# A hybrid decoder block: the parameter chain loaded first and put on VectorE, the mixers' steps in another order, narrow PSUM outputs in the mixers

## The chip, the cores and the metric

The kernel runs on one core of one Trainium2 chip. The metric is the device time of one execution in microseconds (us). The core's engines are TensorE (PE in the profile, PEld for its weight loads), VectorE (DVE), ScalarE (ACT), GpSimd (POOL) and SyncE (SP, which issues most of the DMAs here). Every engine works through its own instructions strictly in order; they meet through semaphores.

## The reference, cut to what matters

One block over 256 positions with 2048 channels, fp32:

```python
proj = rmsnorm(x, norm1_g) @ w_in              # 2048 -> 3072: rg_u, rg_gate, s5_u
y_rg = rg_lru_group(rg_u, rg_gate, ...)        # conv of 4 taps, two gates per head, linear scan, gelu gate
y_s5 = s5_group(s5_u, s5_log_dt, s5_a_re, ...) # 64 groups of 64 complex states, linear scan, GLU
mixed = concat([rmsnorm(y_rg), rmsnorm(y_s5)])
x = x + mixed @ w_out                          # 2048 -> 2048
x = x + conv_gated_mlp(rmsnorm(x), ...)        # 2048 -> 2 x 6144 -> 2048, conv of 3 taps
return rmsnorm(x, final_norm_g)
```

The S5 group's state decays by `exp(A dt)` with `dt = exp(log_dt)`: a chain of small calculations on the parameters (an exponential, an angle reduced to one turn, sines, powers) comes before its first scan.

## The kernel before

**Products.** The activations lie with channels on partitions and 256 positions along the free axis. A product is one tile of 128 output channels: 16 steps of 128 input rows for w_in (24 tiles: 8 of rg_u, 8 of the gate, 8 of s5_u), 8 steps for each half of w_out (16 tiles by two halves) and for w_glu (8 tiles). fp32 accuracy comes from a split: the loaded weights `raw` are rounded into `wh` by ScalarE (`part`, L151) and `wl = raw - wh` is made by VectorE (L154); x is split in the same way. A step (`step`, L156 to L163) adds wh x_high, wh x_low and wl x_high. A *wide* step does the first two with one matmul of 512 columns into both halves of a PSUM bank (L159) and the third with one of 256 (L163); a *narrow* step puts all three into one half with three matmuls of 256 columns (L161 to L163). After a wide product `total` (L165 to L171) must add the two halves: a ScalarE copy (L169) and a VectorE add (L170). A narrow one is read from PSUM as it is. The string `WIDE` says, by letter, which products are wide; before, all of them are but w_down's last tile.

**Steps of the mixers.** Each has a letter and a tile number. U: a tile of rg_u with its convolution; P: its two gates; B: decay and input of the recurrence for four tiles; G: the gate's tile, the recurrence and their product; S: a tile of s5_u; X: the sines of the parameter chain; T (`s5_tables`): cosines and sines at every block of four positions for tile c, six GpSimd multiplications and additions (L495 to L497, each line for two results); K (`s5_mats`): the matrices of tile c, GpSimd work on `ball` (L515 to L517) and on `cp` (L524 to L528), then transposes `tp` (L535) and products `cb` (L541) on TensorE and eight small DMAs `u4` on SP's queue; N (`s5_scan`): `bu` on TensorE (L562) and ten or so VectorE instructions up to `wx` (L578, L579); Y (`s5_out`): the answers `y` on TensorE (L589 to L597) and one VectorE instruction (L599); F: gelu; Z: split; L: a tile of w_glu; W: the first half of a w_out tile; E: W's result times the norm and plus x; V: the second half; R, Q: the two norms' factors (`ss`, a square root, a reciprocal, `rb`). `ball` and its temporaries have one buffer, `cp` and its companions two, so K of tile c + 2 writes `cp` only behind Y of tile c.

**Parameter chain.** `exp_parts` (L324 to L366) makes dt from log_dt with some 50 small instructions on GpSimd; GpSimd goes on with the angles (L371 to L392), ScalarE makes the sines, VectorE prepares their arguments (up to L408) and does a second chain (L410 to L470).

**What sets the order.** The program is written as the steps stand in the string `ORDER`; that sequence gives each instruction its priority, and a scheduler that simulates the engines lays out each engine's own sequence from these priorities. The parameter chain is raised by a fixed offset (PRI). So an entry's place in ORDER is no time; it decides who goes first when an engine could take either.

The weights stream through four `raw` buffers, three of `wh` and of `wl`, by SP's queue. Behind the last V product the FFN follows with 96 + 16 longer products.

Of the kernel before, what the change touches and what calls it, by code (L numbers as in the profile page):

```python
# [14 lines left out]
P = 128  # L15
# [8 lines left out]
NST = 32  # L24
# [5 lines left out]
# The mixers' steps in the order of their priority: a letter of block_kernel's steps and a tile's number.  # L30
ORDER = """
U0 P0 S0 U1 P1 U2 S1 X0 U3 T0 T1 P2 P3 U4 U5 S2 B0 U6 P4 U7 S3 P5 S4 K0 P6 P7 T2 B1 K1 N0 N1 Y0 S5 T3 Y1 F0 G0
K2 G1 G2 S6 T4 G3 G4 K3 F1 N2 T5 Y2 N3 G5 G6 Y3 F2 G7 S7 F3 K4 N4 R0 K5 N5 W0 Y4 T6 W1 W2 Y5 K6 Z0 Z1 E0 E1 W3
E2 E3 Z2 K7 Z3 F4 W4 E4 F5 W5 E5 N6 W6 E6 W7 E7 T7 W8 E8 N7 Y6 W9 Y7 W10 W11 E9 Z4 F6 E10 E11 Z5 W12 F7 E12 Z6
Z7 L0 W13 E13 L1 W14 E14 L2 L3 W15 L4 E15 L5 L6 L7 Q0 V0 V1 V2 V3 V4 V5 V6 V7 V8 V9 V10 V11 V12 V13 V14 V15
"""
# The columns of w_in that the first loads feed, and the order of those loads: a quarter of x or a block of w_in.
# [11 lines left out]
def _top(v, bits):  # L49
# [10 lines left out]
    ("g1", KX), ("g2", KX), ("gf", KX),  # L60
# [3 lines left out]
    ("logdt", NST), ("lam", KH), ("are", NST), ("aim", NST),  # L64
    ("step", NX + NY), ("ident", P),
]
COL = {}
# [8 lines left out]
def block_kernel(ctx, tc, a, out):  # L76
# [9 lines left out]
    # ---------------------------------------------------------------- constants  # L86
    par = cpool.tile([P, NCOL], F32, name="par")
    S.dma_start(par[:, :KX], a["par"][:, :KX])
# [13 lines left out]
    WIDE = "FDAWVL"  # L102
# [13 lines left out]
    def fn(out, src, func, **kw):  # L116
        """An activation that needs its own table: these stay in program order, so that equal ones are neighbours."""
        ins = S.activation(out, src, func, **kw).ins  # L118
        if last_fn:
            tc.add_manual_dep(ins, last_fn[0].name, mybir.DependencyInfo(  # L120
                mybir.DependencyClass.NoSync, mybir.DependencyReason.DATA), reason="table order")
        last_fn[:] = [ins]

    # ------------------------------------------------------------- weight stream
    due = []

    def later(n, fn):
        """fn is emitted behind n more products."""
        due.append([n, fn])
# [26 lines left out]
    def step(ps, wide, wh, wl, kk, x, first, last):  # L156
        """Adds w.T x of 128 rows; wide puts w_high x_low beside the rest."""
# [15 lines left out]
    def product(src, ot, kcs, xs, wide=False):  # L173
        """w.T x; a caller that wants it in PSUM takes the narrow one."""
# [27 lines left out]
    def rstd(parts_, dim, tag):  # L202
        """1 / rms over the channels for every position, on all partitions; without a tag it stays in PSUM."""
# [17 lines left out]
    def rstd_direct(acc, dim, tag):  # L221
        """The same with one step on the tensor engine, more on the vector engine."""
# [17 lines left out]
    # ------------------------------------------------------------- split x  # L240
    # products that nobody reads raise the tensor engine's clock while the first loads run
# [5 lines left out]
    for name in HEAD_LOADS.split():  # L247
        if name == "p":
            nc.sync.dma_start(par[:, KX:], a["par"][:, KX:])
            continue  # L250
# [13 lines left out]
    # ===================================================================== mixers  # L264
    with ExitStack() as ph:
# [3 lines left out]
        # the first columns' products take turns by the rows of x, as these arrive  # L269
# [26 lines left out]
        # short steps let the chain of small ones on the parameters through  # L296
        pieces[0] = CUT

        # -------------------------------------------------- small parameter math
        ahead = tc.high_priority(offset=PRI)  # L300
        ahead.__enter__()
        # what the scans' tiles hold before them
# [12 lines left out]
        def stt(e, out, x, c, y, op0, op1):  # L315
            """(x op0 c) op1 y"""
# [46 lines left out]
        p0, s0, s1 = exp_parts(G, e_in, nE, "d")  # L363
        ex = tl(nE, "ex")
        stt(G, ex, p0, 1.0, s0, ALU.add, ALU.mult)
        G.tensor_tensor(ex, ex, s1, ALU.mult)  # L366
# [6 lines left out]
        # angle of one step, into [-pi, pi]  # L373
# [9 lines left out]
        # angle of a block of steps, in turns, as a short part and its rest; the four state tiles of a channel tile as s5_scan has them  # L383
# [9 lines left out]
        # cosine and sine at the multiples of NY blocks and at those below it  # L393
# [29 lines left out]
        # decay of a block, in s5_scan's order of the state tiles  # L423
# [7 lines left out]
        # powers 3, 2, 1 of A  # L431
# [13 lines left out]
        def times(ore, oim, xre_, xim_, yre, yim, t):  # L445
            """A product of complex numbers; t has the place of two."""
# [9 lines left out]
        # factors of b by the position in the block: A^(3 - position) (A - 1) / a; the real part negated as well  # L456
# [16 lines left out]
        # ------------------------------------------------------------ S5, by tile  # L473
        # Each block of positions is one step of the state's recurrence, in a frame that turns with it.
        # The four state tiles of a channel tile, 2 h + g, lie by g and then h.
        # The imaginary parts of b and of the state are carried negated.
        # What is zero off the diagonal: b [imaginary, tile, channel], c A^3 to c [power, imaginary, tile, channel],
        # the answers to u at the same block's positions [distance, channel]; and the decays, zero at the first block.
# [7 lines left out]
        def s5_tables(c):  # L486
            """Cosine and sine at every block."""
# [12 lines left out]
        def s5_mats(c):  # L500
# [7 lines left out]
            # b for the four positions, [imaginary, tile, channel, position]  # L508
# [386 lines left out]
```

## Time and profile before

| | us |
|---|---|
| median of 3 runs (lowest to highest) | 1183.16 (1183.14 to 1184.67) |
| profiled execution, span on the core | 1181.2 |
| TensorE busy in the span | 1119.9 (95%) |
| VectorE busy | 892.4 (76%) |
| ScalarE busy | 641.0 (54%) |
| GpSimd busy | 270.8 (23%) |

The span of the profiled execution is the time from its first to its last recorded instruction; the median of the runs lies 2.0 us above it, for what happens around it. Busy time is the time in which an instruction is recorded on the engine. A row of a timeline gives the start of an instruction, its duration, the engine, the line of the kernel, the operation, the tiles (output, then inputs), the shape, how many neighbours of the same kind are put together, and in brackets how long the engine was idle before and what released it. The table by windows gives for each engine the busy time and, in brackets, the number of instructions in the window, then the granted TensorE clock as a share of full speed, the share of the DMA engines' time and GB/s.

### The profile page before, as it was taken

To read this page: it belongs to the slowest core of one execution; us is meant where nothing else is said; L and a number is where in the kernel's file an instruction comes from. 1 tells how busy PE (TensorE), PEld (TensorE's weight loads), DVE (VectorE), ACT (ScalarE), POOL (GpSimd) and SP (SyncE) were. 2 spreads that over 40 slices of the span, in tenths; PEclk is the share of its full clock that TensorE was granted. 3 is DMA by queue.
4 is the path that set the end of the run, shared out by engine and by line. 5 is a ranking of instruction groups with operands and counts; after the bars stand their busy time and mean duration, and the time that the engine had idled before them with its cause. 6 is when DMAs were issued, how large, how long until landed. Compare 5 with 4: busy or idle time off the path is not lost.

```text
span 1181.2 us, 18986 instructions
## 1 busy us (share of the span) xinstructions
PE 1119.9 (95%) x7134; PEld 973.9 (82%) x7134; DVE 892.4 (76%) x1356; ACT 641.0 (54%) x1014; POOL 270.8 (23%) x300
## 2 busy tenths in 40 slices
PE   7887869879999999999999999999999999999996
PEld 6775658767888888888888888888888888888886
DVE  6899999997899887787787777877876444445443
ACT  6475655534876655555555555555554444344432
POOL 6368997893333000000000000000000000000000
PEclk8999889999999999999999999999999999999998
DMA  7554336443656666666666666666666666666662
GB/s 255 163 168 136 109 118 195 143 131 99 196 178 191 187 193 189 189 193 186 191 193 187 190 194 186 192 192 187 192 191 185 189 184 187 187 186 190 183 191 90
DMA packets 65980, 209.25 MB, mean 177 GB/s; under 512 B 12000, under 2 KB 15584, under 8 KB 65888
## 3 DMA queue, kind: packets, MB, share of 16 engines
q1 hardware_dynamic: 65744, 208.03, 58.5%
q8 instruction: 56, 0.92, 0.3%
q14 instruction: 36, 0.29, 0.1%
q10 hardware_dynamic: 144, 0.01, 0.0%
HBM read 204.87 MB, written 2.10 MB: 175 GB/s over the span
## 4 chain that ended last, share of the span: by engine, by line
PE 80%; POOL 9%; DVE 7%; issue 2%; ACT 1%; DMA 1%; SPq 0%; DVEq 0%; POOLq 0%; ACTq 0%
PE ps L159 51%; PE ps L163 27%; DVE wl L154 2%; POOL cp L528 1%; DVE wa L574 1%; POOL m L516 1%; POOL ball L517 1%; DVE xq L685 1%; ACT wh L151 1%; DMA xq<-in_xT 1%; POOL m L515 1%; POOL m L525 0%; PE ps L162 0%; DVE rcv L643 0%; PE ps L161 0%
## 5 line engine op out<-in xcount | busy, mean ns | idle before, releaser
L159 PE MATMUL ps<-sp,wh 128*128 128x512 f32 x2960 | 1043.9, 396 | 3.8 <-ACT wh L151 1.9
L163 PE MATMUL ps<-sp,wl 128*128 128x256 f32 x3008 | 851.3, 283 | 18.2 <-DVE wl L154 18.2
L159 PEld LDWEIGHTS ps<-sp,wh 128*128 128x128 f32 x2960 | 558.4, 189 | 130.0 <-DVE sp L199 2.5
L154 DVE TENSOR_TENSOR wl<-raw,wh 128x1024 fp32r<-128x1024 f32 (+2 forms) x384 | 478.5, 1248 | 234.4 <-ACT wh L151 232.7
L151 ACT CAST wh<-raw 128x1024 fp32r<-128x1024 f32 (+1 forms) x378 | 395.0, 1046 | 411.2 <-PE ps L159 286.2
L163 PEld LDWEIGHTS ps<-sp,wl 128*128 128x128 f32 x3008 | 572.3, 190 | 25.9 <-DVE wl L154 23.7
L236 POOL TENSOR_TENSOR accx<-accx,sq 128x256 f32<-128x256 f32 x29 | 37.7, 1301 | 793.6 <-ACT sq L235 793.5
L770 DVE SCALAR_TENSOR_TENSOR cv<-u,par,cv 128x255 f32<-128x255 f32 x192 | 92.1, 481 | 3.7 <-ACT cv L768 0.3
L170 DVE TENSOR_TENSOR t<-t,ps 128x256 f32<-128x256 f32 x160 | 65.7, 412 | 0.1
L169 ACT COPY t<-ps 128x256 f32<-128x256 f32 x160 | 57.8, 363 | 10.0 <-DVE u L720 7.6
L768 ACT ACTIVATE cv<-u,par 128x256 f32<-128x256 f32 x96 | 57.1, 596 | 1.4 <-DVE u L766 1.4
L766 DVE TENSOR_TENSOR u<-t,rstd 128x256 f32<-128x256 f32 x96 | 40.4, 421 | 1.6
L528 POOL TENSOR_TENSOR cp<-m,m 64x192 f32<-64x192 f32 x32 | 31.1, 973 | 1.9
L788 DVE TENSOR_TENSOR xq<-xq,ps 128x256 f32<-128x256 f32 x31 | 13.0, 421 | 16.4 <-PE ps L163 15.9
L721 POOL TENSOR_TENSOR xq<-xq,u 128x256 f32<-128x256 f32 x16 | 18.0, 1127 | 26.4 <-DVE u L720 20.8
L118 ACT ACT_TABLE_LOAD x17 | 21.8, 1283 | 1.4 <-PEq L884 1.2
L780 DVE TENSOR_TENSOR hv<-ge,cv 128x256 f32<-128x256 f32 x48 | 20.4, 426 | 1.9 <-issue 0.2
L118 ACT ACTIVATE ge<-cv 128x256 f32<-128x256 f32 x48 | 20.1, 419 | 0.2
L193 DVE TENSOR_TENSOR sp<-hv,sp 128x256 fp32r<-128x256 f32 x48 | 20.1, 419 | 0.0
L531 ACT COPY bp<-ball 64x128 f32<-64x128 f32 x16 | 6.8, 423 | 24.3 <-POOL ball L517 24.2
L192 ACT CAST sp<-hv 128x256 fp32r<-128x256 f32 x48 | 19.5, 406 | 0.0
L199 DVE SCALAR_TENSOR_TENSOR sp<-xq,par,sp 128x256 fp32r<-128x256 f32 x32 | 15.6, 521 | 1.5 <-ACT sp L198 1.5
(245 smaller groups left out, 654.2 us busy)
## 6 DMA issues: line engine op xcount, KB each, us to landing
raw<-in_w_up SPq DMA_DIRECT2D x192, 512.0 KB, 4.3
raw<-in_w_down SPq DMA_DIRECT2D x96, 512.0 KB, 4.3
raw<-in_w_in SPq DMA_DIRECT2D x47, 512.0 KB, 4.2
raw<-in_w_out SPq DMA_DIRECT2D x32, 512.0 KB, 4.1
raw<-in_w_glu SPq DMA_DIRECT2D x8, 512.0 KB, 4.1
xq<-in_xT SPq DMA_DIRECT2D x7, 512.0 KB, 6.0
out_y<-xq SPq DMA_DIRECT2D x6, 256.0 KB, 2.1
rw<-in_rgw SPq DMA_DIRECT2D x8, 128.0 KB, 3.5
```

The lines of the kernel that those rows point to most:

```text
L118: ins = S.activation(out, src, func, **kw).ins
L151: S.copy(wh[:, k, :], raw[:, k, :])
L154: V.tensor_tensor(wl[:, i:i + n, :], raw[:, i:i + n, :], wh[:, i:i + n, :].bitcast(F32), ALU.subtract)
L159: PE.matmul(ps, lhsT=wh[:, kk, :], rhs=x, start=first, stop=False)
L163: PE.matmul(ps[:, 0, :], lhsT=wl[:, kk, :], rhs=x[:, 0, :], start=False, stop=last)
L169: S.copy(t, ps[:, 1, :])
L170: V.tensor_tensor(t, t, ps[:, 0, :], ALU.add)
L236: G.tensor_tensor(acc, acc, q, ALU.add)
L528: G.tensor_tensor(cp[rp, :BL - 1, m, :, 16 * h:16 * h + 16], m1[rp], m2[rp], op)
L766: V.tensor_tensor(u, ps, rs["n2"], ALU.mult)
L768: S.activation(cv, u, AF.Identity, bias=col("fcb", o), scale=col("fcw", 2 * 2 * KF + o))
L770: V.scalar_tensor_tensor(cv[:, d:], u[:, :T - d], col("fcw", (2 - d) * 2 * KF + o), cv[:, d:], ALU.mult, ALU.add)
```

## The change

1. The columns of `par` are reordered. The first DMA (ScalarE's queue) loads the norm's gains and now log_dt, lambda, the real and imaginary parts of A and the step numbers with them (136 columns instead of 16); the rest follows on SP's queue with 632 columns instead of 752, at the same place.
2. `exp_parts` and the two instructions behind it get `V` (VectorE) where they had `G` (GpSimd).
3. `ORDER` is another sequence.
4. `WIDE` keeps only the FFN's letters: the 24 products of w_in, the 32 of w_out and the 8 of w_glu become narrow, 64 in all, and lose L169 and L170. What read `t` reads PSUM.

Comments and docstrings go too, and all line numbers from L88 on rise by one.

```diff
 ORDER = """
-U0 P0 S0 U1 P1 U2 S1 X0 U3 T0 T1 P2 P3 U4 U5 S2 B0 U6 P4 U7 S3 P5 S4 K0 P6 P7 T2 B1 K1 N0 N1 Y0 S5 T3 Y1 F0 G0
-K2 G1 G2 S6 T4 G3 G4 K3 F1 N2 T5 Y2 N3 G5 G6 Y3 F2 G7 S7 F3 K4 N4 R0 K5 N5 W0 Y4 T6 W1 W2 Y5 K6 Z0 Z1 E0 E1 W3
...
+U0 X0 S0 P0 U1 P1 T0 K0 U2 P2 S1 N0 Y0 U3 P3 B0 T1 K1 U4 P4 S2 N1 Y1 U5 P5 T2 K2 U6 P6 S3 N2 Y2 U7 P7 B1 T3 K3 F0
+F1 F2 G0 S4 N3 Y3 F3 T4 K4 G1 G2 S5 N4 Y4 F4 T5 K5 G3 G4 S6 N5 Y5 F5 T6 K6 G5 G6 S7 N6 Y6 F6 T7 K7 G7 N7 Y7 F7 R0
...
-    ("g1", KX), ("g2", KX), ("gf", KX),
+    ("g1", KX), ("logdt", NST), ("lam", KH), ("are", NST), ("aim", NST), ("step", NX + NY),
+    ("g2", KX), ("gf", KX),
...
-    ("logdt", NST), ("lam", KH), ("are", NST), ("aim", NST),
-    ("step", NX + NY), ("ident", P),
+    ("ident", P),
...
+NFIRST = KX + 3 * NST + KH + NX + NY
...
-    S.dma_start(par[:, :KX], a["par"][:, :KX])
+    S.dma_start(par[:, :NFIRST], a["par"][:, :NFIRST])
...
-    WIDE = "FDAWVL"
+    WIDE = "FD"
...
-            nc.sync.dma_start(par[:, KX:], a["par"][:, KX:])
+            nc.sync.dma_start(par[:, NFIRST:], a["par"][:, NFIRST:])
...
-        p0, s0, s1 = exp_parts(G, e_in, nE, "d")
+        p0, s0, s1 = exp_parts(V, e_in, nE, "d")
         ex = tl(nE, "ex")
-        stt(G, ex, p0, 1.0, s0, ALU.add, ALU.mult)
-        G.tensor_tensor(ex, ex, s1, ALU.mult)
+        stt(V, ex, p0, 1.0, s0, ALU.add, ALU.mult)
+        V.tensor_tensor(ex, ex, s1, ALU.mult)
```

Three places show what the scheduler makes of it. First GpSimd at the start of the program, between the sums of squares of x (`acc_130`, L289) and the angles (`room`, L371 before, L372 after). Before:

```order
L289 TENSOR_TENSOR acc_130<-acc_130,q 128x1024
L332 TENSOR_SCALAR room<-room 128x40
L333 TENSOR_SCALAR room<-room 128x40
L334 TENSOR_SCALAR room<-room 128x40
L321 TENSOR_SCALAR room<-room 128x40
L349 TENSOR_SCALAR room<-room 128x40
```

The exponential begins there and the first angle instruction stands 28 rows further on. On the same engine after:

```order
L290 TENSOR_TENSOR acc_130<-acc_130,q 128x1024 x2
L372 TENSOR_TENSOR room<-par,room 128x32
L373 TENSOR_TENSOR room<-par,room 128x32
L376 TENSOR_SCALAR room<-room 128x32
L377 TENSOR_SCALAR room<-room 128x32
```

The exponential has left GpSimd; the angles stand right behind the sums, and wait for VectorE's dt.

Second TensorE around the first W products. Before, the matrices of tile 4 (`cb_2416`, `bu_2438`) stand inside W1 (`ps_2637`):

```order
L159 MATMUL ps_2637<-sp_2166,wh_2640 128x512
L541 MATMUL cb_2416<-cp0_511,bp0_510 32x96 x8
L562 MATMUL bu_2438<-u4_2429,bt_2414 64x64 x16
L163 MATMUL ps_2637<-sp_2166,wl_2641 128x256
L159 MATMUL ps_2637<-sp_2227,wh_2640 128x512
L163 MATMUL ps_2637<-sp_2227,wl_2641 128x256
L159 MATMUL ps_2637<-sp_2326,wh_2640 128x512
```

The same engine after, at the first W product (`ps_3223` is W0, `ps_3070` is G7, `bu_3144` belongs to tile 7, the last):

```order
L162 MATMUL ps_3070<-sp_315,wh_3103 128x256
L163 MATMUL ps_3070<-sp_315,wh_3103 128x256
L164 MATMUL ps_3070<-sp_315,wl_3104 128x256
L563 MATMUL bu_3144<-u4_3061,bt_3046 64x64 x16
L162 MATMUL ps_3223<-sp_1827,wh_3226 128x256
L163 MATMUL ps_3223<-sp_1827,wh_3226 128x256
L164 MATMUL ps_3223<-sp_1827,wl_3227 128x256
```

Before, W0 to W9 stand between the matrices of tiles 4 to 7; after, no W product stands ahead of the last matrices, and the gates' products G0 to G7 with S5 to S7 fill those places.

Third TensorE and VectorE around the answers of tile 3 (`y_1923`) and the matrices of tile 4 (`cb_2007`), after. TensorE:

```order
L542 MATMUL cb_2007<-cp0_571,bp0_570 32x96 x4
L162 MATMUL ps_2177<-sp_133,wh_2180 128x256
L590 MATMUL y_1923<-wx_1912,cp1_579 32x64 x8
L593 MATMUL y_1923<-us3_1523,cb1_580 128x192
L593 MATMUL y_1923<-us3_1523,cb1_580 128x128
L593 MATMUL y_1923<-us3_1523,cb1_580 128x64
L598 MATMUL y_1923<-wx_1912,cp1_579 32x63 x24
```

and VectorE, where `y_1923` is read:

```order
L155 TENSOR_TENSOR wl_2181<-raw_2178,wh_2180 128x1024
L600 SCALAR_TENSOR_TENSOR us2_1171<-us2_1171,par_70,y_1555 128x256
L155 TENSOR_TENSOR wl_2211<-raw_2208,wh_2210 128x1024
L155 TENSOR_TENSOR wl_2380<-raw_2377,wh_2379 128x1024
L600 SCALAR_TENSOR_TENSOR us3_1523<-us3_1523,par_70,y_1923 128x256
L673 TENSOR_SCALAR q4_1670<-e4_1669 128x1024
L674 TENSOR_SCALAR e4_1669<-tau_1102 128x1024
```

The answers of a tile stand on TensorE behind the `cb` of the next tile, which is the last thing that the next tile's GpSimd work feeds; on VectorE the weights' subtractions of later products stand behind the instruction that reads these answers. The same pattern repeats at tiles 0, 2, 4 and 5.

## Rows read from the trace of the kernel before

**Rows 1.** Page: span, and shares of the chain that ended last

```profile
span 1181.2 us, 18986 instructions
...
PE 80%; POOL 9%; DVE 7%; issue 2%; ACT 1%; DMA 1%; SPq 0%; DVEq 0%; POOLq 0%; ACTq 0%
```

**Rows 2.** Windows: start, end, length, busy (count) PE PEld DVE ACT POOL, PEclk, DMA

```profile
0.00:60.00 60.00, 49.55 (x252) 41.46 (x253) 44.18 (x115) 32.40 (x49) 31.79 (x69) 0.94 0.62 208
```

**Rows 3.** Windows: from the first table to the last K; all mixers

```profile
70.30:271.70 201.40, 161.58 (x1469) 133.03 (x1468) 189.53 (x244) 110.46 (x210) 182.06 (x185) 0.93 0.44 135
...
0.00:364.30 364.30, 313.10 (x2459) 263.22 (x2460) 327.60 (x528) 215.32 (x394) 246.87 (x282) 0.95 0.51 158
```

**Rows 4.** TensorE's waits before 360 us: engine, line, releaser, total, times, longest

```profile
PE ps L163 <- DVE wl L154: 18.2, 17, 3.1
PE cb L541 <- POOL cp L528: 8.8, 3, 6.6
```

**Rows 5.** Timeline of POOL: first angle, first table, first K, end of the last K

```profile
33.28 0.25 POOL L371 TENSOR_TENSOR room<-par,room 128x32 f32<-128x32 f32 x1
...
70.33 0.70 POOL L496 TENSOR_TENSOR tm<-xs 128x256 f32<-128x256 f32 x1
...
91.73 0.65 POOL L515 TENSOR_TENSOR m<-pk,fr 128x256 f32<-128x256 f32 x1 [2.73 <-DVE fr L451]
...
270.12 1.60 POOL L528 TENSOR_TENSOR cp<-m,m 64x192 f32<-64x192 f32 x2
```

**Rows 6.** Timeline of DVE and ACT: the sines' argument, a small instruction, the sines

```profile
61.82 0.40 DVE L408 TENSOR_SCALAR xs<-xs 128x512 f32<-128x512 f32 x1
62.15 0.17 DVE L418 TENSOR_TENSOR room<-room 128x32 f32<-128x32 f32 x1
...
68.33 1.28 ACT L118 ACT_TABLE_LOAD   x1
69.62 0.63 ACT L118 ACTIVATE xs<-xs 128x512 f32<-128x512 f32 x1
```

**Rows 7.** Timeline of PE: W0; matrices of K4; answers; a V product; FFN

```profile
218.19 0.48 PE L159 MATMUL ps<-sp,wh 128*128 128x512 f32 x1
...
224.37 0.54 PE L541 MATMUL cb<-cp,bp 128*32 128x96 f32 x16
224.84 0.69 PE L562 MATMUL bu<-u,bt 64*64 64x64 f32 x32
...
284.67 0.43 PE L589 MATMUL y<-wx,cp 128*32 128x64 f32 x16
...
286.74 0.39 PE L163 MATMUL ps<-sp,wl 128*128 128x256 f32 x1
...
333.78 0.39 PE L159 MATMUL ps<-sp,wh 128*128 128x512 f32 x1
...
336.56 0.39 PE L159 MATMUL ps<-sp,wh 128*128 128x512 f32 x1
...
364.29 0.39 PE L159 MATMUL ps<-sp,wh 128*128 128x512 f32 x1
```

**Rows 8.** Narrow steps of w_down's last tile (durations, starts); two wide starts, 48 steps apart

```profile
L161 PE MATMUL ps<-sp,wh x48: 279/279/279, 1152.1 to 1168.7; 128*128 128x256 f32 x48
...
1119.63 0.40 PE L159 MATMUL ps<-sp,wh 128*128 128x512 f32 x1
...
1136.59 0.40 PE L159 MATMUL ps<-sp,wh 128*128 128x512 f32 x1
```

**Rows 9.** Windows with L154 alone: with GpSimd busy beside it, and without

```profile
70.00:272.00 202.00, 64.98 (x40) 0.93 0.44 134
600.00:800.00 200.00, 88.55 (x73) 1.00 0.65 190
```

**Rows 10.** Windows with L170 alone, the same two stretches

```profile
70.00:272.00 202.00, 10.12 (x25) 0.93 0.44 134
600.00:800.00 200.00, 14.91 (x36) 1.00 0.65 190
```

More of the change, by code (lines that the diff above doesn't have):

```diff
@@ L31 @@
 ORDER = """
-U0 P0 S0 U1 P1 U2 S1 X0 U3 T0 T1 P2 P3 U4 U5 S2 B0 U6 P4 U7 S3 P5 S4 K0 P6 P7 T2 B1 K1 N0 N1 Y0 S5 T3 Y1 F0 G0
-K2 G1 G2 S6 T4 G3 G4 K3 F1 N2 T5 Y2 N3 G5 G6 Y3 F2 G7 S7 F3 K4 N4 R0 K5 N5 W0 Y4 T6 W1 W2 Y5 K6 Z0 Z1 E0 E1 W3
-E2 E3 Z2 K7 Z3 F4 W4 E4 F5 W5 E5 N6 W6 E6 W7 E7 T7 W8 E8 N7 Y6 W9 Y7 W10 W11 E9 Z4 F6 E10 E11 Z5 W12 F7 E12 Z6
-Z7 L0 W13 E13 L1 W14 E14 L2 L3 W15 L4 E15 L5 L6 L7 Q0 V0 V1 V2 V3 V4 V5 V6 V7 V8 V9 V10 V11 V12 V13 V14 V15
+U0 X0 S0 P0 U1 P1 T0 K0 U2 P2 S1 N0 Y0 U3 P3 B0 T1 K1 U4 P4 S2 N1 Y1 U5 P5 T2 K2 U6 P6 S3 N2 Y2 U7 P7 B1 T3 K3 F0
+F1 F2 G0 S4 N3 Y3 F3 T4 K4 G1 G2 S5 N4 Y4 F4 T5 K5 G3 G4 S6 N5 Y5 F5 T6 K6 G5 G6 S7 N6 Y6 F6 T7 K7 G7 N7 Y7 F7 R0
+W0 Z0 Z1 E0 W1 Z2 Z3 E1 W2 Z4 Z5 E2 W3 Z6 Z7 E3 L0 L1 W4 E4 L2 L3 W5 E5 L4 L5 W6 E6 L6 L7 W7 E7 W8 E8 W9 E9 Q0 W10
+E10 W11 E11 W12 E12 W13 E13 W14 E14 W15 E15 V0 V1 V2 V3 V4 V5 V6 V7 V8 V9 V10 V11 V12 V13 V14 V15
 """
```

## The prediction

> **What bounds the kernel now.** The page comes first: a span of 1181.2 us, and on the chain that ended last PE has 80%, POOL 9% and DVE 7% [rows 1]. POOL does nothing in the FFN, so its 9% lie in the mixers. The table by windows says where: of the first 60 us PE is busy for 49.55 and DVE for 44.18 [rows 2]; over the whole mixers, which end with the first FFN matmul at 364.29 [rows 7], PE is busy for 313.10 of 364.30 us [rows 3]. Between the first table (70.33) and the end of the last K (271.7) POOL is busy for 182.06 of 201.40 us and DVE for 189.53 [rows 3, 5]: here these two set the pace and PE follows. The table of PE's waits says the same: wl of DVE holds it 17 times, 18.2 us in all, and cp of POOL 8.8 us [rows 4]. PE's own clock is part of it: 0.93 in that stretch, 1.00 where it is always fed. After 364.3 nothing changes. So the whole prediction is the time at which the mixers end, T, and the time after is T + (1181.2 - 364.3) + 2.0 = T + 818.9; the 2.0 are what the median, 1183.16, has over the span.
>
> **Part 1: parameters first, exponential on DVE.** The longer first load moves 128 x 120 x 4 bytes = 61 KB more ahead; at the 208 GB/s of the first 60 us [rows 2] that is 0.3 us on another queue, while DVE still has nothing to split. Taken as nothing. POOL loses the exponential and had dt ready at 33.28 [rows 5]. DVE gains 51 instructions of 40 elements. Its small ones take 0.17 us [rows 6], so 8.7 us, in a stretch in which it was idle for 60 - 44.18 = 15.8 us [rows 2]: that idle time is the cover, and without it the weights behind the chain come up to 8.7 us later. When do the sines come? DVE's sequence now has 124 instructions up to the sines' argument (which started at 61.82 [rows 6]): 51 small ones, 8.7 us, and 73 others at the mean 44.18/115 = 0.384, 28.0 us. With all of the 15.8 us idle that is 52, with none 37; I take 50, since part of the old idle time was waiting that the chain now fills. The sines follow (0.63 us each with their hand-overs, and no load of a table directly ahead, which cost 1.28 [rows 6]): 3 us. **The tables start at 53** instead of 70.33, between 47 and 60. The first K follows 21 POOL instructions later, at about 74 instead of 91.73.
>
> **Part 2: the order.** What a 17 us earlier start is worth is decided by what stands behind it. Before, W0 starts at 218.19 [rows 7], and ten W products lie between the matrices of the last four tiles, so PE has work while POOL finishes. After, no W product stands ahead of the last matrices. All 40 w_out and w_glu products come behind one point, W0, and T is W0 plus their work. So POOL's rate fixes W0. From the first table to the end of K6 it has 160 instructions. At 182.06/185 = 0.984 us each [rows 3] they take 157.5 and end at 210.5; at 201.40/185 = 1.089, the old waits included, 174 and 227. Part of the old waits were for the old order's interleaving, but the new one has waits of its own (below). I take the middle, **219**.
>
> From K6's end to W0 PE has, in its order: cb 0.5, 46 matmuls of 256 columns, the answers of tile 5, 63 matmuls, bu, tp, 26 matmuls, cb, 22 matmuls, bu. A matmul of 256 columns is a third of a narrow step, and a step is 16.6/47 = 0.353 [rows 8], so 0.118; cb and bu are 0.5 and 0.7, the answers 286.74 - 284.67 = 2.1 [rows 7], tp like cb. Sum: 157 x 0.118 = 18.5, and 5.0 for the rest: 23.5. Added wait: the answers of tile 5 need N5, whose last instruction is DVE's 209th from the start of the tables. At DVE's 189.53/244 = 0.777 that is 215, at 201.40/244 = 0.825 it is 225.5; PE wants it at 225. But in the new order DVE also waits: the reading of y_1923 stands ahead of the rest on DVE, y_1923 stands on PE behind cb of K4, and that behind POOL; queued behind it on DVE are B1, u and wl of the next w_in products, for which PE waits in turn. I take 4 (0 to 9). **W0: 219 + 23.5 + 4 = 246.5.**
>
> From W0 on PE is fed: 40 products of 8 steps, 336.56 - 333.78 = 2.78 each [rows 7], 111.2; two sets of answers, 4.1; the two norms' small matmuls, like two bu, 1.4. W3's wl stands on DVE behind the reciprocal of R, and this behind the answers of tile 7, a square root and a table load: an estimate of 5 us (3 to 8) in which PE has nothing else. Sum 121.7, and **T = 368.2**, where it was 364.3: the 17 us of earlier tables go into 40 products that no longer fill gaps.
>
> **Part 3: narrow outputs.** PE: a narrow step of 0.353 [rows 8] against wide ones of 2.78/8 = 0.3475 in the mixers [rows 7]. Over 704 steps the difference is 3.9 us; but in the same place as the narrow steps, 48 wide ones take 1136.59 - 1119.63 = 16.96, again 0.353 [rows 8]. That row is the nearest; I take nothing and keep 0 to 4, and no gain, for the columns are the same. DVE and ACT lose 64 additions and copies; the additions took 10.12/25 = 0.405 [rows 10], 26 us in all. From W0 on PE is the bound and these are covered. Before W0 DVE loses 24 of them, which is in the count of 209 already.
>
> Does a lighter DVE make POOL quicker? wl, which reads raw and wh, takes 64.98/40 = 1.62 beside a busy POOL and 88.55/73 = 1.21 without one [rows 9]; L170, which reads t and a PSUM bank, 0.405 and 14.91/36 = 0.414 [rows 10]. So the removed additions were not in POOL's way. But u, the product of t and rstd1, now reads PSUM in place of t, and becomes such an instruction. (The Trainium skill, page "SBUF — State Buffer", section "Who interferes with whom", says it as a rule: a VectorE instruction with two SBUF inputs contends with a GpSimd one that reads SBUF, the pair of ports being held for the whole instruction; one with a single SBUF input does not. The two rows agree with it in kind; by it the 64 additions gave POOL nothing, and the sum stands, while the u's help it, which is the first rival.)
>
> **Rivals.**
> *Faster: the u's stop blocking POOL.* Some 18 u's lie between the first table and K6's end. If each cost POOL its whole duration, of the size of L170's 0.41, K6 ends 18 x 0.41 = 7.4 us earlier, at 211.6, and DVE is early enough for the answers of tile 5 (the 4 us go): 1187.1 - 11.4 = 1175.7, say **1176**. With the half of the waits that I kept gone as well, 1168. It decides when K6 ends before 212.7, since the time is K6's end + 968.1. For it: [rows 9, 10]. Against it: 7.4 us is a bound, for POOL is not beside every u, and the B1 and N instructions are as many as before.
> *No change:* K6 ends between 212.7 and 217.4: 1180.8 to 1185.5. It needs only 2 to 6 us from my 219, well inside its ends.
> *The chain does not come earlier.* DVE's head is busier than I think, the sines wait for it as before (61.82), the tables start at 60: 7 us later, **1194**; with POOL's slower rate, 227, it is 1202. It is the case in which the change doesn't do what it says. Against it: DVE's idle 15.8 us.
> *Narrow steps cost PE* the upper bound, 320 x 0.0055 = 1.8 us behind W0: **1189**.
>
> **How the numbers follow.** The forecast is 219 + 968.1 = **1187**, with the slower neighbours up to 1194 (also the narrow steps): 0.37. The chain late or POOL at its slow rate, 1194 and over: 0.13. No change: 0.18. Faster: 0.32. A measurement of this kernel can tell about 0.2%, 2.4 us, from no change, so the bounds are 1180.8 and 1185.5: faster 0.32, same 0.18, slower 0.50. Of the faster case little lies below 1168 (0.08) and of the slow one about as much above 1202; the range is 1168 to 1202. The forecast's own range is 1185 to 1194.
>
> **What will show it.** In the changed kernel's profile: the first table on POOL at 53 (47 to 60); the first K at 74; the last instruction of K6 at 219 and of K7 at about 237; DVE idle for several us ahead of the reading of tile 3's answers; the first W product on PE at 246.5, right behind a bu; from there 122 us with PE solid but for a hole of about 5 us ahead of W3; the first FFN product at 368. No copy or addition of two PSUM halves before the FFN, and the FFN as long as before, 816.9 us. The prediction is wrong if K6 ends before 213 (POOL or its waits cheaper than counted), if PE waits much longer than 4 us for tile 5's answers, or if a narrow step shows over 0.353 at full clock.

## The result

The changed kernel takes 1194.66 us (median of four runs, 1192.53 to 1195.09) against 1183.74 us before: a ratio of 1.0085, 95% interval 1.0071 to 1.0100. It is slower by 10.9 us, where 4 were forecast. In the profiled execution the first FFN matmul starts at 373.9 us instead of 364.3 [rows 7], and the FFN takes what it took: 1190.7 - 373.9 = 816.8 us. So the loss lies in the mixers, as the forecast had it, and it is larger.

The page of the changed kernel, span and chain, to be read beside [rows 1]; DVE has 9% of the chain and POOL 5%, where it was 7% and 9%:

```profile
span 1190.7 us, 20225 instructions
...
PE 81%; DVE 9%; POOL 5%; issue 2%; ACT 1%; DMA 1%; SPq 0%; DVEq 0%; POOLq 0%; ACTq 0%
```

Its timeline of POOL (start, duration, engine, line, operation, tiles; lines are one higher than before): the first table, the first instruction of the first K, the last one of tile 6 and of tile 7. They answer to [rows 5].

```profile
49.96 0.89 POOL L497 TENSOR_TENSOR tm<-xs 128x256 f32<-128x256 f32 x1 [13.48 <-ACT xs L119]
...
73.24 1.87 POOL L516 TENSOR_TENSOR m<-pk,fr 128x256 f32<-128x256 f32 x1 [2.96 <-DVE fr L452]
...
217.46 1.26 POOL L529 TENSOR_TENSOR cp<-m,m 64x192 f32<-64x192 f32 x2
...
234.66 2.14 POOL L529 TENSOR_TENSOR cp<-m,m 64x192 f32<-64x192 f32 x2
```

The tables start 20 us earlier than before, and the last K ends at 236.8 instead of 271.7. And yet the mixers end 9.6 us later. PE's timeline shows the rest: the last bu and W0 behind it, rb and W3, the first step of V1 and the first of V2 (8 steps later), the first FFN matmul. They answer to [rows 7].

```profile
247.22 1.24 PE L563 MATMUL bu<-u,bt 64*64 64x64 f32 x32
248.39 0.39 PE L162 MATMUL ps<-sp,wh 128*128 128x256 f32 x1
...
263.36 0.71 PE L215 MATMUL rb<-par,rs 128*128 128x128 f32 x4 [1.11 <-DVE rs L212]
264.09 0.39 PE L162 MATMUL ps<-sp,wh 128*128 128x256 f32 x1
...
330.73 0.28 PE L162 MATMUL ps<-sp,wh 128*128 128x256 f32 x1
...
333.61 0.28 PE L162 MATMUL ps<-sp,wh 128*128 128x256 f32 x1
...
373.93 0.40 PE L160 MATMUL ps<-sp,wh 128*128 128x512 f32 x1
```

A narrow product of 8 steps takes 333.61 - 330.73 = 2.88 us here; the wide one took 2.78 [rows 7].

Two views account for the 9.6 us. The first is the table by windows from PE's first product (7 us) to the first third matmul of the FFN, 364.5 before and 374.2 after (start, end, length, then busy time and count of PE, PEld, DVE, ACT, POOL, the granted clock, DMA share, GB/s). Before:

```profile
7.00:364.50 357.50, 308.46 (x2435) 258.75 (x2436) 325.31 (x522) 211.48 (x388) 242.74 (x267) 0.95 0.51 157
```

After:

```profile
7.00:374.20 367.20, 325.03 (x3140) 309.17 (x3141) 315.03 (x486) 194.76 (x328) 224.24 (x240) 0.93 0.48 154
```

PE is idle for 49.0 us before and 42.2 after, so it gained 6.8 there; but it is busy for 16.6 us more. By an estimate, about 7 of these are clock (0.95 against 0.93, 0.02 of 367 us: more of the time at the lower of the two levels, 1.2 instead of 2.4 GHz), and about 9 the narrow steps, 704 x 0.0125 = 8.8 (0.360 us for a narrow step here, 0.3475 for a wide one). The second view is the same table with the third matmul of a step alone (L163 before, L164 after), whose count is the number of steps done. Before:

```profile
0.00:120.00 120.00, 66.07 (x222) 43.68 (x222) 0.96 0.56 178
120.00:180.00 60.00, 25.98 (x86) 17.80 (x87) 0.88 0.40 124
180.00:240.00 60.00, 33.84 (x118) 22.33 (x117) 0.97 0.53 165
```

After:

```profile
0.00:120.00 120.00, 55.95 (x183) 38.61 (x183) 0.91 0.50 164
120.00:180.00 60.00, 26.85 (x85) 18.49 (x85) 0.87 0.40 123
180.00:240.00 60.00, 30.43 (x101) 20.66 (x100) 0.91 0.43 135
```

By 240 us PE had done 426 of the mixers' 704 steps before, and 369 after: 57 steps, 20 us, fewer, 39 of them by 120 us already. The window up to there, before and then after:

```profile
0.00:240.00 240.00, 197.67 (x1473) 163.62 (x1473) 216.21 (x349) 136.84 (x240) 186.80 (x221) 0.94 0.51 161
...
0.00:240.00 240.00, 197.94 (x1938) 183.88 (x1942) 208.39 (x346) 123.28 (x213) 189.36 (x217) 0.90 0.46 147
```

PE was busy equally long, so the earlier matrices had brought no idle time back by then. By an estimate from these rows, the lower clock takes half of the 20 us (0.04 x 240 = 9.6), the price of the narrow steps 4.6 (369 x 0.0125), and only the rest, some 6 us, is the matrices and answers of early tiles, which PE did ahead of products. That part is not lost, since it need not be done later, and the 6.8 us of idle time are won behind 240 us; so the end moves by less than the 20 us.

### The profile page after: what moved, and what is told of

The parts are those of the page before. It is cut to its first block, busy times and chain, and to the rows that moved or that the text cites. A ratio compares the mean times of both kernels' runs of the same rounds, so it can differ in the third digit from the quotient of the medians.

```text
span 1190.7 us, 20225 instructions
## 1 busy us (share of the span) xinstructions
PE 1136.6 (95%) x7838; PEld 1024.5 (86%) x7838; DVE 878.0 (74%) x1318; ACT 622.4 (52%) x947; POOL 247.2 (21%) x270
## 3 DMA queue, kind: packets, MB, share of 16 engines
q1 hardware_dynamic: 65744, 207.97, 54.3%
## 4 chain that ended last, share of the span: by engine, by line
PE 81%; DVE 9%; POOL 5%; issue 2%; ACT 1%; DMA 1%; SPq 0%; DVEq 0%; POOLq 0%; ACTq 0%
PE ps L160 43%; PE ps L164 27%; PE ps L162 4%; PE ps L163 4%; DVE wl L155 2%; POOL cp L529 1%; DMA xq<-in_xT 1%; DVE xq L686 1%; DVE rcv L644 1%; POOL ball L518 1%; DVE wa L575 1%; POOL m L516 1%; POOL m L517 1%; DVE sp L200 0%; POOL m L525 0%
## 5 line engine op out<-in xcount | busy, mean ns | idle before, releaser
L164 PE MATMUL ps<-sp,wl 128*128 128x256 f32 x3008 | 855.9, 285 | 13.9 <-DVE wl L155 13.9
L160 PE MATMUL ps<-sp,wh 128*128 128x512 f32 x2256 | 787.1, 393 | 0.0
L164 PEld LDWEIGHTS ps<-sp,wl 128*128 128x128 f32 x3008 | 577.3, 192 | 17.0 <-DVE wl L155 15.8
L160 PEld LDWEIGHTS ps<-sp,wh 128*128 128x128 f32 x2256 | 422.6, 187 | 95.6
L162 PE MATMUL ps<-sp,wh 128*128 128x256 f32 x752 | 222.3, 296 | 7.3 <-ACT wh L152 4.6
L163 PE MATMUL ps<-sp,wh 128*128 128x256 f32 x752 | 221.2, 294 | 0.1
L162 PEld LDWEIGHTS ps<-sp,wh 128*128 128x128 f32 x752 | 151.8, 202 | 9.8 <-ACT wh L152 5.8
L163 PEld LDWEIGHTS ps<-sp,wh 128*128 128x128 f32 x752 | 151.6, 202 | 0.9 <-DVE sp L200 0.5
L171 DVE TENSOR_TENSOR t<-t,ps 128x256 f32<-128x256 f32 x96 | 39.7, 413 | 0.0
L170 ACT COPY t<-ps 128x256 f32<-128x256 f32 x96 | 34.7, 361 | 0.0
L529 POOL TENSOR_TENSOR cp<-m,m 64x192 f32<-64x192 f32 x32 | 26.4, 825 | 4.9 <-PE y L598 3.0
L200 DVE SCALAR_TENSOR_TENSOR sp<-xq,par,sp 128x256 fp32r<-128x256 f32 x32 | 21.9, 703 | 0.5 <-ACT sp L199 0.5
L781 DVE TENSOR_TENSOR hv<-ge,cv 128x256 f32<-128x256 f32 x48 | 20.4, 425 | 1.7
```

Of the source, the lines that this page charges most:

```text
L160: PE.matmul(ps, lhsT=wh[:, kk, :], rhs=x, start=first, stop=False)
L162: PE.matmul(ps[:, 0, :], lhsT=wh[:, kk, :], rhs=x[:, 0, :], start=first, stop=False)
L163: PE.matmul(ps[:, 0, :], lhsT=wh[:, kk, :], rhs=x[:, 1, :], start=False, stop=False)
L164: PE.matmul(ps[:, 0, :], lhsT=wl[:, kk, :], rhs=x[:, 0, :], start=False, stop=last)
L171: V.tensor_tensor(t, t, ps[:, 0, :], ALU.add)
L529: G.tensor_tensor(cp[rp, :BL - 1, m, :, 16 * h:16 * h + 16], m1[rp], m2[rp], op)
```

## The experiments

Two theories stood against each other. The first is the prediction's: the earlier chain is a gain, the new order turns it into a loss since all 40 products of w_out and w_glu stand behind one point, and the narrow outputs cost a little PE time where PE is the bound. The rival: the order is harmless, and narrow outputs or the meeting of VectorE and GpSimd make the time. All ratios are to the kernel before on the same chip.

| kernel | us | ratio, 95% interval | mixers' end | w_up |
|---|---|---|---|---|
| before | 1183.74 | | 364.5 | 533.4 |
| chain alone | 1182.75 | 0.9995 (0.9986 to 1.0004) | 365.3 | 533.5 |
| order alone | 1208.43 | 1.0209 (1.0193 to 1.0225) | 380.2 | 543.4 |
| narrow alone | 1181.86 | 0.9990 (0.9979 to 1.0000) | 363.6 | 533.5 |
| chain, order | 1204.94 | 1.0176 (1.0160 to 1.0191) | 376.6 | 543.4 |
| chain, narrow | 1180.14 | 0.9970 (0.9953 to 0.9987) | 362.4 | 533.5 |
| chain, w_in narrow | 1180.78 | 0.9967 (0.9954 to 0.9980) | 362.0 | 533.5 |
| chain, order, w_in narrow | 1200.54 | 1.0148 (1.0133 to 1.0163) | 372.5 | 543.4 |
| the change: chain, order, narrow | 1194.66 | 1.0085 (1.0071 to 1.0100) | 374.2 | 533.5 |
| the change with a third order | 1193.43 | 1.0078 (1.0061 to 1.0095) | 374.2 | 533.5 |

The mixers' end is the start of the FFN's first third matmul, w_up the time from there to w_down's, both from the traces. Four pairs of rows differ by the order alone, and in all four it makes the mixers longer: 364.5 to 380.2, 365.3 to 376.6, 362.4 to 374.2, and 362.0 to 372.5, which is 10 to 16 us. Of the eight combinations of the three parts, order with narrow outputs alone was not run.

**Each part alone.** The chain alone: the changed kernel with the old order (its beginning is shown) and wide mixers:

```diff
-U0 X0 S0 P0 U1 P1 T0 K0 U2 P2 S1 N0 Y0 U3 P3 ...
+U0 P0 S0 U1 P1 U2 S1 X0 U3 T0 T1 P2 P3 U4 U5 ...
...
-    WIDE = "FD"
+    WIDE = "FDAWVL"
```

> The kernel before with the parameter chain of the change alone: parameters first, exponential on VectorE; old order, wide mixers. Theory (the chain is a gain and the order gives it away): the first table starts at about 50 as in the changed kernel instead of 70.3, W products still lie between the last matrices, the mixers end 8 to 20 us earlier than 364.3, time 1164 to 1176. Rival (GpSimd and VectorE set the pace and an earlier start only makes them meet more often): the tables start early, the last K ends within 3 us of 271.7, time 1181 to 1187.

Measured: no difference, 0.9995. The step that failed is the start of the tables. In POOL's timeline it is 67.07, not 50:

```profile
67.07 0.67 POOL L497 TENSOR_TENSOR tm<-xs 128x256 f32<-128x256 f32 x1 [0.41 <-ACT xs L119]
```

In the old order X0 stands behind the first gates. The sines' argument is ready on VectorE at 51.6, but ScalarE is busy with the gates and with weights until 65.1 and only then turns to the sines. The order alone (next) starts the tables at 65.6. With both, the chain and X0's place, they start at 54.3, and at 50 with the narrow outputs too. The last K ends at 270.3 (271.7 before).

The order alone:

```diff
-U0 P0 S0 U1 P1 U2 S1 X0 U3 T0 T1 P2 P3 U4 U5 ...
+U0 X0 S0 P0 U1 P1 T0 K0 U2 P2 S1 N0 Y0 U3 P3 ...
```

> The kernel before with the new order alone; chain on GpSimd, wide mixers. Theory (40 products behind one point W0, and W0 set by GpSimd): first table at 65 to 70, W0 as much later than in the changed kernel (248.4) as the tables are, 263 to 268, then 40 products of 2.78 and some 10 us of the rest, mixers end at 385 to 390, time 1204 to 1209. Rival (the order is harmless, and the loss is the narrow outputs'): 1181 to 1187.

Measured: 1208.43, the theory's number, but not for its reasons: the mixers end at 380.2 and not at 385 to 390, w_up takes 10 us longer, which nobody had expected (below), and W0 starts at 243.5 and not at 263 to 268. It stands there ahead of the last tile's matrices, whose bu comes at 257.7. The steps done, third matmul alone, show where the mixers lose:

```profile
0.00:120.00 120.00, 67.18 (x227) 45.52 (x227) 0.94 0.56 181
120.00:180.00 60.00, 26.20 (x88) 16.98 (x87) 0.94 0.43 123
180.00:240.00 60.00, 19.20 (x64) 13.03 (x63) 0.83 0.33 97
```

Up to 180 us the new order is ahead (315 steps against 308); from 180 to 240 it does 64 where the old one does 118, with the granted clock at 0.83. That is the stretch of the matrices of tiles 4 to 6, in which the old order has the last w_in products and, from 218 us on, W products for PE.

The narrow outputs alone:

```diff
-    WIDE = "FDAWVL"
+    WIDE = "FD"
```

> The kernel before with narrow mixers alone; old chain, old order. Theory (a narrow step costs TensorE 0.360 against 0.3475 us where it is the bound, and VectorE's relief buys nothing): from 270.9 on some 30 products of 8 steps, 3.0 us, and as much again at most before; time 1185 to 1190. Rival (VectorE and GpSimd meet less often, since u reads PSUM): the last K ends 5 to 8 us earlier, time 1176 to 1181.

Measured: 1181.86, 0.9990, neither of the two. The last K ends at 265.2, 6.5 us earlier, as the rival has it, though half of that is an earlier first table (67.1 instead of 70.3); the mixers end only 0.9 us earlier. The window from PE's first product to the mixers' end:

```profile
7.00:363.60 356.60, 317.17 (x3138) 302.52 (x3138) 308.41 (x466) 195.69 (x328) 242.44 (x269) 0.95 0.50 157
```

PE is idle for 39.4 us instead of 49.0, and busy for 8.7 more. Both theories hold in part and cancel: the narrow outputs give 9.6 us of idle time back, and the 704 narrow steps, at the same granted clock, take 8.7 more.

**Pairs.** Chain and order, wide mixers:

```diff
-    WIDE = "FD"
+    WIDE = "FDAWVL"
```

> The changed kernel with all mixers wide again: chain and order of the change. Theory (a narrow step costs 0.0125 us where TensorE is the bound, VectorE's relief nothing): W0 within 3 us of 248.4, 4.0 us less behind it, time 1188 to 1193. Rival (narrow outputs make GpSimd quicker ahead of W0): W0 5 us or more later, time 1196 or above.

Measured: 1204.94, the rival's time but neither side's reason. 10 us of it are w_up's. W0 is neither near 248.4 nor later: it starts at 231.0 and stays open to 263.7, among the last tiles' matrices, whose last bu comes at 256.7. With narrow outputs POOL had tile 6's matrices at 218.7, here at 237.0, though most of that (14 us) is the first K's start, 87.1 against 73.2. What the narrow w_in is worth shows beside the kernel with wide w_out and w_glu (below), which differs by it alone: its mixers end at 372.5 instead of 376.6.

Chain and narrow outputs, old order:

```diff
-U0 X0 S0 P0 U1 P1 T0 K0 U2 P2 S1 N0 Y0 U3 P3 ...
+U0 P0 S0 U1 P1 U2 S1 X0 U3 T0 T1 P2 P3 U4 U5 ...
```

> The changed kernel with the old order: chain and narrow outputs of the change. Theory (the order alone turns the gain into a loss): as the chain alone, 1164 to 1176, and 2 to 4 us on top for the narrow steps, 1167 to 1180. Rival (the order is harmless): 1192 to 1197.

Measured: 1180.14, 0.9970, the theory's sign, at the very edge of its range: without the order the other two parts are a small gain, some 14 us faster than all three. The gain of 8 to 20 us that the theory gave to the chain is not there. Idle time and clock, in the window to the mixers' end:

```profile
7.00:362.40 355.40, 318.89 (x3139) 304.07 (x3138) 308.79 (x485) 195.97 (x328) 231.31 (x239) 0.94 0.50 158
```

PE is idle for 36.5 us, the least of the four kernels whose window is shown. This kernel and its variant with wide w_out and w_glu (below) beat both the kernel before and the changed one. The changed kernel differs from it by the order alone, and the two windows price the order: 5.7 us more of idle time (42.2 against 36.5) and 6.1 us more of busy time (325.0 against 318.9) for the same matmuls, at a granted clock of 0.93 against 0.94. PE's waits for GpSimd's matrices (total, times, longest) show a part of the idle time, first with chain and narrow outputs, then in the changed kernel:

```profile
PE tp L536 <- POOL ball L518: 5.4, 3, 2.5
PE cb L542 <- POOL cp L529: 1.9, 2, 1.2
...
PE cb L542 <- POOL cp L529: 8.1, 5, 3.0
PE tp L536 <- POOL ball L518: 5.6, 5, 2.3
```

That is 13.7 us instead of 7.3; the waits for wl rise as well, from 9.5 to 13.9, while those for wx fall from 9.0 to 1.4. That these waits are the cause, and what lowers the clock, no run shows by itself.

The change with wide w_out and w_glu:

```diff
-    WIDE = "FD"
+    WIDE = "FDWVL"
```

> The changed kernel with the w_out and w_glu products wide again (40 products), w_in narrow. Theory (the slope behind W0 is the narrow step's): 2.78 instead of 2.88 us per product behind W0, 4.0 us, time 1190 to 1192. Rival (another cause slows TensorE there, such as the transfers or VectorE): 2.88 stays, time 1194 to 1197 with the additions back.

Measured: 1200.54, and both readings fail. The 40 products do cost less: from the start of W0 to the mixers' end it is 3.8 us shorter (2.82 per product up to the second norm, 2.77 behind it, instead of 2.88). But W0 starts 2.1 us later, and so the mixers end at 372.5 instead of 374.2. Against that, w_up takes 543.4 us instead of 533.5. The whole loss, and more, is in code that is the same in both kernels.

**The price of a narrow step by itself.** w_up narrow, then w_down narrow, in the kernel before:

```diff
-    WIDE = "FDAWVL"
+    WIDE = "DAWVL"        (or "FAWVL")
```

> The kernel before with the 96 products of w_up narrow (16 steps each, 1536 steps), mixers as before. It measures the price of a narrow step by itself, where TensorE is always the bound. Theory (0.360 against 0.347 us wherever the clock is full): 1536 x 0.0125 = 19 us, time 1200 to 1205. Rival (the price of w_down's last tile, 0.353, holds and the mixers' 0.360 is the mixers' own): 1536 x 0.0055 = 8 us, 1190 to 1193; second rival (nothing, since wide and narrow are equal in w_down): 1182 to 1185.

> The kernel before with all of w_down narrow (15 more tiles of 48 steps, 720 steps). There wide steps take 0.353 and the narrow ones of the last tile, where hardly any transfer runs, 0.353 too. Theory A (a narrow step takes 0.360 beside running transfers and split work): 720 x 0.007 = 5 us, 1187 to 1190. Theory B (w_down's narrow steps take 0.353 everywhere in it): no change, 1182 to 1185.

Measured: 1200.50, 1.0140 (1.0125 to 1.0155), and 1183.50, 1.0004 (0.9994 to 1.0015). PE in a window of w_up, narrow:

```profile
400.00:600.00 200.00, 200.00 (x1669) 200.00 (x1668) 143.48 (x209) 100.88 (x139) 0.00 (x0) 1.00 0.56 183
```

1669/3 = 556 steps in 200 us, 0.3595 each; the kernel before does 1156/2 = 578 in the same window, 0.3460. The whole of w_up took 20.4 us longer (553.8); the total rose by only 17.3, since w_down, which is the same in both, took 267.8 us instead of 271.0 (see the pace below). PEld, the loading of weights, is busy for all of the 200 us. In w_down, narrow:

```profile
920.00:1100.00 180.00, 180.00 (x1530) 180.00 (x1529) 81.73 (x75) 75.36 (x84) 14.02 (x10) 1.00 0.59 186
```

510 steps in 180 us, 0.353, as its wide steps had (1021 matmuls in that window, 0.353). PEld is busy throughout here too. So theory A falls: it is not the running transfers (DMA share 0.56 and 0.59) that make a narrow step slow. A narrow step takes 0.360 in the mixers and in w_up and 0.353 in w_down; why w_down's are quicker was not found. (The Trainium skill, page "TensorE: Matmul & The Clock Gate", section "Back-to-back issue gap", gives 262 cycles for an isolated matmul of 256 columns and 518 for one of 512; by an estimate from these a narrow step would cost 6 cycles more than a wide one, 2.5 ns. The runs show 13 in w_up and none in w_down, and the measurement decides.)

**The pace of wide steps.** In three kernels all of w_up runs slower by 10 us. PE in the same window, order alone:

```profile
400.00:600.00 200.00, 200.00 (x1134) 173.45 (x1133) 157.89 (x254) 116.13 (x183) 0.00 (x0) 1.00 0.64 186
```

and the changed kernel:

```profile
400.00:600.00 200.00, 200.00 (x1156) 176.34 (x1155) 159.41 (x253) 115.03 (x181) 0.00 (x0) 1.00 0.59 190
```

1134 matmuls against 1156 at the same full clock: 353 ns per wide step against 346. To learn whether this is a state or a property of the program, matmuls that nobody reads were put between products of w_up, in the kernel with chain and order and in the one before:

```diff
         for j in range(KF):
+            if j in (8, 16, 24, 32, 40):
+                wz2 = ps1.tile([P, P], F32, tag="y", name="wz2")
+                for _ in range(j // 8):
+                    PE.matmul(wz2, lhsT=ones, rhs=ones, start=True, stop=True)
             cg = up(j)
```

> A probe of the pace of wide steps in w_up. The kernel with chain and order of the change and wide mixers, whose w_up ran 543.4 us (353 ns per step) instead of 533.4 (347 ns), with 1, 2, 3, 4 and 5 matmuls of 128 columns that nobody reads put ahead of w_up's pairs of products 8, 16, 24, 32 and 40. Theory (the pace is a state of TensorE's stream, set anew by each interruption and kept until the next): at least one of the five stretches behind an interruption runs at 5.55 us per product, the others at 5.65 or another fixed value, with the change at the interruption. Rival (the pace belongs to the program, its buffers' places or its transfers): 5.65 in all stretches.

> The same probe in the kernel before, whose w_up ran 533.4 us (5.55 us per product). Theory (a state set by interruptions): at least one stretch behind an interruption runs at 5.65, time up to 8 us above 1183. Rival (the pace belongs to the program): 5.55 in all stretches, 1183 to 1186.

Measured: 1197.03 and 1182.97 (one run each). The scheduler moved all these matmuls ahead, to 276 to 368 us, since they wait for nothing; so w_up was not interrupted as planned, and the theory and its rival were not put to the test that was meant. The first run tells something all the same: w_up, whose own matmuls are the same, is back to 533.5, with a change of pace in the middle of a product that the trace shows. PE's timeline around rb of the third norm, four matmuls that the scheduler puts into the stream:

```profile
394.92 0.40 PE L160 MATMUL ps<-sp,wh 128*128 128x512 f32 x1
...
395.26 0.40 PE L160 MATMUL ps<-sp,wh 128*128 128x512 f32 x1
...
395.61 0.40 PE L160 MATMUL ps<-sp,wh 128*128 128x512 f32 x1
395.85 0.61 PE L215 MATMUL rb<-par,rs 128*128 128x128 f32 x4
396.21 0.36 PE L164 MATMUL ps<-sp,wl 128*128 128x256 f32 x1
396.42 0.40 PE L160 MATMUL ps<-sp,wh 128*128 128x512 f32 x1
396.65 0.28 PE L164 MATMUL ps<-sp,wl 128*128 128x256 f32 x1
396.77 0.40 PE L160 MATMUL ps<-sp,wh 128*128 128x512 f32 x1
```

Ahead of rb the steps start 0.34 to 0.36 apart in a pattern of three (mean 353 ns), behind it 0.347, and so to the end of w_up. In the kernel without the added matmuls, chain and order, the same rb stands one matmul later, between a third matmul and the next wide one, and the slow pattern goes on behind it:

```profile
393.49 0.28 PE L164 MATMUL ps<-sp,wl 128*128 128x256 f32 x1
393.61 0.60 PE L215 MATMUL rb<-par,rs 128*128 128x128 f32 x4
393.97 0.48 PE L160 MATMUL ps<-sp,wh 128*128 128x512 f32 x1
...
394.40 0.40 PE L160 MATMUL ps<-sp,wh 128*128 128x512 f32 x1
...
394.76 0.40 PE L160 MATMUL ps<-sp,wh 128*128 128x512 f32 x1
```

So the same matmuls of w_up run at either pace at the same granted clock. In both of these traces the pace falls at the third norm's ss; in the probe it rises again at rb, and either pace is then kept to the end of w_up, for 500 us. In six more traces the stream is slow when the FFN begins and quick for the rest of w_up. In four of them (narrow alone, chain and narrow, the change, the third order) the change comes at an ss that stands between a wide matmul and its third. In the other two (chain alone, and chain with w_in narrow, below) it comes at an ss behind a third matmul, ahead of the next wide one. Chain alone:

```profile
375.44 0.28 PE L164 MATMUL ps<-sp,wl 128*128 128x256 f32 x1
375.56 0.50 PE L208 MATMUL ss<-ones,accx 128*128 128x1 f32 x4
375.92 0.48 PE L160 MATMUL ps<-sp,wh 128*128 128x512 f32 x1
```

The steps start 353 ns apart ahead of it and 347 behind it. The three slow kernels have ss split into two pairs, behind which the pace fell, and rb ahead of a wide matmul. In the kernel with wide w_out and w_glu an ss between a wide matmul and its third, at 313.6 us, left the slow pace as it was. So no one place of the interruption goes with one pace in all traces, and no run moved it alone: that the pace changed at the norm's matmuls is shown, what sets it is open. Nor does a change need other matmuls: in the kernel before the steps go from 347 to 353 ns with w_down's first product, at 898 us, and nothing but products stands there. In p_before, and with w_up narrow, w_down took 267.8 us instead of 271.0.

**Wide tail, old order; and a third order.** The chain, w_in narrow, the rest wide, old order (`WIDE = "FDWVL"`):

> Old order, the change's chain, w_in narrow, w_out and w_glu wide. The kernel with all narrow has 1180.1. Theory (a narrow step costs where TensorE is the bound): the 24 or so products behind the last K cost 0.1 us less each, mixers end at 359 to 360 instead of 362.4, time 1176 to 1179, if w_up keeps its pace of 533.4; if its pace falls, 10 us more, 1186 to 1189, and the mixers' end tells which. Rival (VectorE's additions in the tail eat it): mixers end at 362 or later, 1180 to 1184.

Measured: 1180.78, 0.9967 (0.9954 to 0.9980): the same as with all narrow, and the mixers' end, 362.0, is 0.4 us earlier, not 2 to 3. The last K ends at 267.0 instead of 264.0, so what the tail's wide products save is not won at the end. The rival's side.

The changed kernel with the change's order up to tile 3's matrices, then gates early and W products between the matrices of tiles 5 to 7:

```diff
-F1 F2 G0 S4 N3 Y3 F3 T4 K4 G1 G2 S5 N4 Y4 F4 T5 K5 G3 G4 S6 N5 Y5 F5 T6 K6 G5 G6 S7 N6 Y6 F6 T7 K7 G7 ...
+F1 F2 G0 S4 N3 G1 T4 Y3 G2 K4 F3 G3 G4 T5 S5 G5 N4 G6 K5 Y4 G7 S6 F4 R0 N5 W0 T6 S7 W1 K6 Y5 W2 ...
```

> The changed kernel with a third order: the change's up to the matrices of tile 3, then the gates' products early and W0 to W9 between the matrices of tiles 5 to 7, as in the old order. Theory (the loss is that all 40 products stand behind W0, whatever comes ahead): K3 ends near 154 as in the changed kernel, W products run ahead of the last K, mixers end at 355 to 365 instead of 374.2, time 1172 to 1186. Rival (an early start of the matrices only moves TensorE's idle time, and the w_in products it displaces come later): 370 or more, 1190 or above.

Measured: 1193.43; the mixers end at 374.2, as in the changed kernel. The theory that the 40 products behind W0 are the loss fails here: the last K ends at 264.1, W products run ahead of it, and nothing is won. Steps done:

```profile
0.00:120.00 120.00, 55.72 (x183) 38.12 (x183) 0.93 0.51 164
120.00:180.00 60.00, 28.11 (x91) 19.14 (x91) 0.86 0.41 123
180.00:240.00 60.00, 28.55 (x97) 19.51 (x96) 0.88 0.48 153
```

371 by 240 us against the changed kernel's 369, and again 183 by 120. W0 starts at 238.5, 20 us later than before, since it needs the gate's eight products and w_in's products are late from the first 120 us on. What the two new orders share is the beginning, up to tile 3's matrices; that the loss lies there is likely by these rows, but no run changed the beginning alone.

## Why the prediction was right, and where it was off

The time lies inside the range and on the forecast side; the forecast, 1187, is 7.6 us short of 1194.7. The sum is met nearly term by term, but two terms came out by luck, one was mis-sized, and its account of where the loss comes from is only partly borne out.

- **Start of the tables and of K0**: 53 and 74 were forecast, 49.96 and 73.24 came. The sum over VectorE's sequence held. That it was the chain's doing was part of it: chain alone gives 67.07 and order alone 65.6.
- **POOL from the tables to K6**: 219 forecast, 218.7 measured, K7 at 236.8 against 237. In the window between them its 160 instructions (the last engine in the row) were busy for 149.81 of 168.7 us, 0.936 each instead of the 0.984 of the lower bound, and the waits, 18.9 us, made up for it. That the middle of two rates came out is in part luck. First the changed kernel, then the one with chain, order and wide mixers, from its first table to its tile 6:

```profile
50.00:218.70 168.70, 137.91 (x1428) 127.15 (x1427) 144.93 (x196) 83.89 (x150) 149.81 (x160) 0.88 0.40 126
...
54.30:237.00 182.70, 142.93 (x1258) 116.13 (x1257) 163.59 (x224) 94.85 (x179) 151.68 (x162) 0.92 0.43 132
```

The first rival's mechanism, u without its second SBUF operand, would make POOL's instructions shorter, and it does not show: with wide mixers, where u reads two operands from SBUF, they take 151.68/162 = 0.936 as well. (By the rule of the Trainium skill's page "SBUF — State Buffer", section "Who interferes with whom", a VectorE instruction with two SBUF inputs contends with a GpSimd one that reads SBUF, so the narrow outputs would help POOL; the two rows show nothing of it in the mean instruction.) What differs between the two rows are POOL's waits, 18.9 us instead of 31.0.
- **K6 to W0**: 27.5 forecast, 29.7 measured, W0 at 248.4 instead of 246.5. The wait for tile 5's answers was 1.4 us, not 4; PE itself came late to K6's cb, at 221.9.
- **W0 to the mixers' end**: 121.7 forecast, 125.5 measured. The hole ahead of W3 was at the low end of its 3 to 8 us: PE waits about 2 us around rb, and behind it the clock falls to its lower level for 3.4 us, which costs half of the 2.95 us that PE is busy there:

```profile
264.90:268.30 3.40, 2.95 (x14) 2.95 (x15) 3.40 (x6) 1.61 (x3) 0.00 (x0) 0.50 0.56 161
```

- **The term that was mis-sized is the narrow step.** Nothing was taken, with 1.8 us behind W0 as the bound; 40 x (2.88 - 2.78) = 4.0 came. The row that was called nearest, w_down's own steps [rows 8], was near by its shape only: in w_down the wide steps too run at the slower pace, 0.353, and so the two forms look equal there. The mixers' narrow steps run at 0.360, which no narrow row of before showed, and the bound from [rows 8] excluded it. A narrow step over 0.353 at full clock was one of the prediction's own signs of being wrong, and it came.
- **"After 364.3 nothing changes"** held, 816.8 us for the FFN, but by luck: three of the kernels above have 10 us more in w_up with the same code there, and nothing in the prediction's rows says which pace the changed kernel gets. (That POOL does nothing in the FFN is not so: it is busy for 270.8 us in all and for 246.87 up to 364.3 [rows 3], which leaves 24. No term hangs on it.)
- The rest of the miss, 2 us, is not in the trace: the profiled execution took 1192.53, the quickest of the four, and the median is 1194.66.
- **"The 17 us go into 40 products that no longer fill gaps"** has the right sign and is not borne out as the cause. That the order is what costs is shown by the four pairs. That PE lacks products between the matrices holds for the order alone between 180 and 240 us. In the changed kernel G products fill that stretch, and the steps are behind earlier, half of them by a lower clock; bringing W products forward won nothing. What PE waits for in its first 120 us there, one releaser after the other, was not taken apart by an experiment.
- **DVE's idle time ahead of the reading of tile 3's answers** was forecast as a sign. DVE is idle there, but the 4.87 us are a wait of wl for ScalarE's wh, one instruction ahead; the answers themselves hold it for 0.47.
- The rival of late tables (1194) has the measured time, but not its cause: the tables were early.

## What to carry to other kernels

Where an engine with the most work is fed by a slower side chain, look at that engine and not at the end of the side chain: split its time up to the end of the stage into idle time, busy time and granted clock. Here the last matrices came 35 us earlier and the end 10 us later. A count of the steps done shows where an engine falls behind, but does not rank kernels: with chain and order 389 steps are done by 240 us, 20 more than in the changed kernel, and its mixers end 2.4 us later. Test a bundle by its parts and pairs: two parts of this one together are a gain of 0.3%, and the third turns that into a loss of 0.85%. A form of instruction is priced from a place where it runs under the same conditions, or the range has to reach to both neighbours.

## What the runs showed of the hardware

- In w_up a stream of alternating matmuls of 512 and 256 columns runs at one of two paces, 346 or 353 ns for a pair at the same granted clock, 1.00, and keeps it from the third norm's matmuls to the end of the 96 products: 533.4 or 543.4 us. What sets the pace is open; it also changes with w_down's first product. Kernels whose mixers differ get 10 us more or less in the FFN by it, so a mixer's edit can't be judged by the total alone.
- Three matmuls of 256 columns with three weight loads take 0.360 us in w_up and 0.353 in w_down, with PEld busy throughout in both, against 0.346 and 0.353 for the wide form.
